# A decoder layer: the order of all engines from the end of the output projection written by hand

## Chip, cores and metric

One core of one Trainium2 chip. The metric is the device time of one launch in microseconds (us); lower is better. A run is one execution; the kernel before has three of them.

## What is computed

One decoder layer for 512 tokens of width 1024, in float32. The part that this change touches begins where the mixers have ended:

```python
def rms_norm(x, g):
    y = x * lax.rsqrt(jnp.mean(x * x, axis=-1, keepdims=True) + 1e-6)
    return y * g
...
x = x + rms_norm(mix @ w_out, post_mix_norm)          # output projection, first norm
h = rms_norm(x, pre_ffn_norm)                         # second norm
f = (jax.nn.silu(h @ w_ffn_gate) * (h @ w_ffn_up)) @ w_ffn_down
x = x + rms_norm(f, post_ffn_norm)
```

Shapes: mix 512x1024, w_out 1024x1024, w_ffn_gate and w_ffn_up 1024x2816, w_ffn_down 2816x1024.

## The kernel before

**Products in three parts.** A matmul operand is kept as a high and a low part (`hi`, `lo`, type fp32r), and a product is three matmuls: hi by hi, hi by lo, lo by hi (L270 to L272). So each weight is split after it has been loaded: ScalarE (ACT) copies it to `whi` and VectorE (DVE) writes `wlo = wraw - whi` (L135, L136). The loads go through the queue of SyncE (SP) into four buffers `wraw`; the split halves have four buffers of their own.

**Output projection and norms.** The tokens are four tiles t = 0 to 3 of 128. `wo_unit(t, i)` multiplies tile t with the i-th of eight row blocks of w_out, 6 matmuls of 512 columns into two PSUM banks (one for each half of the columns). For t = 0 and 1, blocks 0 to 5 run before the stretch shown here, blocks 6 and 7 in it. After the eight blocks of a tile comes `norms(t)`:

- ACT squares each half with a running sum (L252). DVE makes the mean `rs` (L254, L256) and multiplies the half by the gain, `py` (L260). GpSimd (POOL) raises `rs` to the power -1/2 (L258). DVE adds the scaled halves to the residual, `xr` (L264), and SP stores them to `x1d` (L267).
- For the second norm ACT squares `xr` (L863), DVE makes the mean (L224), POOL the power `rstd` (L226), and DVE writes the normed tile `hn` (L865).

`tr(t)` then turns `hn` of tile t on TensorE (PE; eight transposes, L239), ACT and DVE split the result into `h2H` and `h2L` (L127, L128), and ACT keeps a full copy `h2f` (L243). PE runs `tr(0)` inside the eight blocks of t = 2, `tr(1)` before the last block of t = 2, `tr(2)` before the last block of t = 3.

**Gate and up projection.** The first pair of column blocks is multiplied directly, first for tokens 0 to 255 (h2 of t = 0 and 1), gate then up, each in two halves i = 0 and 1 of the inner dimension, 24 matmuls of 256 columns for each; `tr(3)` stands between up i = 0 and up i = 1. Then follow the 96 matmuls for tokens 256 to 511. The remaining ten pairs run as Strassen products: from four blocks A11, A12, A21, A22 of the weights the sums S1 to S4 are formed on DVE (L920), ACT and DVE split seven operands for a pair (`unit_hi`, `unit_lo`, L944 and L952), and each unit is one product of 24 matmuls (L1016). The token side has sums too: T1 to T4 (L975), formed from `h2f` and split into `tH` and `tL`.

**What sets the order.** PE's order is written by hand throughout. The order of ACT, DVE, POOL and SP up to the Strassen products is made by the scheduler of the framework, from the program's order and dependences; from the first product on it is by hand. Each engine takes its instructions strictly in that order, SP its DMA issues too.

Of the kernel before, what the change touches and what calls it, by code (L numbers as in the profile page):

```python
# [18 lines left out]
S = 512  # L19
# [85 lines left out]
def tile_hybrid_layer(ctx: ExitStack, tc: tile.TileContext,  # L105
# [129 lines left out]
    def transpose_half(t, h, dst_hi, dst_lo, dst, half):  # L235
        p = bank("at")
        for c in range(4):
            cc = half * 4 + c
            nc.tensor.transpose(p[:, c * 128:(c + 1) * 128], h[:, cc * 128:(cc + 1) * 128], ident)  # L239
        pv = p.rearrange("p (c n) -> p c n", c=4)  # L240
        sl = (slice(None), slice(half * 4, half * 4 + 4), slice(t * 128, (t + 1) * 128))
        split_psum(pv, dst_hi[sl], dst_lo[sl])
        nc.scalar.activation(dst[sl], pv, AF.Copy)  # L243

    def post_norm(pl, po, xtile, g, dst=None, junk_of=None):
# [3 lines left out]
        for half in range(2):  # L249
            cs = slice(half * 512, (half + 1) * 512)  # L250
            junk = junk_of() if junk_of else pl.tile([128, 512], F32, name="pj")
# [703 lines left out]
    for tok in HALVES:  # L955
        for nm in ("gate", "up"):
            for i in range(2):
                if tok is HALVES[0] and nm == "up" and i == 1:
                    tr(NT - 1)
                part_fm(pss0[nm], (nm, 0), h2H, h2L, i, tok)  # L960
        if tok is HALVES[0]:
            np_.release()
            xres.release()
            gains.release()
            atp = tc.alloc_tile_pool(name="atp", bufs=1, side="left")
            aF = atp.tile([128, NF, S], F32, name="aF")
            for name in LORD:
                load_blk(0, name)
            for u in range(2):
                sums(u)  # L970
                unit_hi(u)
                unit_lo(u)
            B11, B12, B21, B22 = (h2f[:, 4 * k:4 * k + 4, tk] for k in range(2) for tk in HALVES)
            T1, T2, T3, T4 = B12, B22, B11, B21
            tsub = lambda o, a, b: V.tensor_tensor(out=o, in0=a, in1=b, op=ALU.subtract)  # L975
            tsub(T1, B12, B11)
            tsub(T2, B22, T1)
            split_sbuf(T2, tH[:, 1], tL[:, 1])
            split_sbuf(T1, tH[:, 0], tL[:, 0])
            tsub(T3, T2, B11)  # L980
            split_sbuf(T3, tH[:, 2], tL[:, 2])
            tsub(T4, B21, T2)
# [12 lines left out]
    state["fine"] = False  # L995
    for u in range(2, 5):
        sums(u)
        unit_hi(u)
        unit_lo(u)
# [77 lines left out]
    with tc.manual_schedule():  # L1077
        for u in range(NU):
            q, i = divmod(u, len(UORD))
            if i == 0:  # L1080
                cur[q] = dict(A=bank("mm"), B=bank("at"), D=bank("mm"))
            product(cur[q]["ABADADA"[i]], u, i in (0, 1, 3))
            post(u - 1)
            unit_hi(u + 5)
            if u:
                unit_lo(u + 4)
            sums(u + 6)
            if u in (NU - 5, NU - 4, NU - 1):
                pump_load(state["split"] + 4)
                pump_split(state["split"] + 1)  # L1090
            if u == NU - 2:
                split_a(2)
        post(NU - 1)
# [64 lines left out]
```

## Time and profile before

| | us |
|---|---|
| median of 3 runs (lowest to highest) | 602.11 (601.75 to 602.14) |
| the profiled execution, its own time | 604.18 |
| span of its trace, first to last instruction | 602.2 |
| PE busy in the span | 575.9 |
| DVE, ACT, POOL busy | 407.3, 302.2, 43.4 |

A row of a timeline gives start, duration, engine, line, what is written from what, how many merged, and in brackets how long the engine stood idle before it and what released it. Times run from the start of the span. A matmul's end is modelled: consecutive ones overlap, so the distance between their starts is what each costs. The granted clock of PE is given as a share of 2.4 GHz: 1.00 or 0.50 (1.2 GHz), and in between where a stretch holds both.

### The profile page before, as it was taken

The numbers are of one execution on the slowest core, as the hardware profiler recorded it, in microseconds if no ns is written. First come the engines' busy times: TensorE is split into PE (matmuls) and PEld (weight loads), VectorE is DVE, ScalarE is ACT, GpSimd is POOL, SyncE is SP. The second block draws the span as 40 slices with busy tenths as digits, with TensorE's granted clock in tenths as the row PEclk, the third lists the DMA queues.
The fourth block names the chain that finished last, engine by engine and source line by source line (L and its number), as shares of the span: only waits on it lengthen the run. The fifth ranks groups of instructions, "written<-read, shape, count | busy, mean of one in ns | idle before, by whom it ended". The sixth has DMA issues, their size and how long they took to land.

```text
span 602.2 us, 9161 instructions
## 1 busy us (share of the span) xinstructions
PE 575.9 (96%) x3554; PEld 509.2 (85%) x3554; DVE 407.3 (68%) x670; ACT 302.2 (50%) x498; POOL 43.4 (7%) x93
## 2 busy tenths in 40 slices
PE   6999898999898999979999999999999999999995
PEld 5977676888687887879999999999999988888874
DVE  5787386478888845798888788888788533323344
ACT  4656472366788935735455545545554423222231
POOL 3450001201010002010000000000000000000000
PEclk7999988999999999989999999999999999999998
DMA  8456615332322173741234323432314462332002
GB/s 307 127 143 92 147 39 139 89 114 70 97 88 71 52 260 144 220 128 37 71 106 141 106 71 106 140 109 79 112 54 146 155 251 78 106 104 83 23 36 104
DMA packets 67353, 68.45 MB, mean 114 GB/s; under 512 B 4467, under 2 KB 56726, under 8 KB 67310
## 3 DMA queue, kind: packets, MB, share of 16 engines
q1 hardware_dynamic: 66222, 65.24, 34.9%
q0 software_dynamic: 1088, 2.62, 3.0%
q8 instruction: 28, 0.46, 0.3%
q14 instruction: 15, 0.12, 0.1%
HBM read 59.99 MB, written 5.76 MB: 109 GB/s over the span
## 4 chain that ended last, share of the span: by engine, by line
PE 74%; DVE 9%; DMA 7%; ACT 5%; issue 3%; POOL 0%; SPq 0%; DVEq 0%; POOLq 0%; ACTq 0%
PE mm L1016 28%; PE mm L270 7%; PE mm L272 7%; PE mm L271 7%; DMA wraw<-in_w_in_dram 6%; PE mm L299 5%; PE at L1016 5%; PE at L270 4%; PE at L271 4%; PE at L272 4%; DVE wlo L136 3%; DMA wraw<-in_w_ffn_up_dram 1%; DVE h L384 1%; PE at L768 1%; DVE kz L687 1%
## 5 line engine op out<-in xcount | busy, mean ns | idle before, releaser
L136 DVE TENSOR_TENSOR wlo<-wraw,whi 128x512 fp32r<-128x512 f32 (+2 forms) x88 | 70.2, 820 | 53.7 <-ACT whi L135 53.6
L135 ACT ACTIVATE whi<-wraw 128x512 fp32r<-128x512 f32 (+3 forms) x92 | 63.4, 721 | 68.9 <-PE mm L272 29.6
L1016 PE MATMUL mm<-tH,wlo 128*128 128x256 f32 x240 | 67.9, 283 | 0.0
L1016 PE MATMUL mm<-tH,whi 128*128 128x256 f32 x240 | 67.8, 283 | 0.0
L1016 PE MATMUL mm<-tL,whi 128*128 128x256 f32 x240 | 67.8, 282 | 0.0
L1016 PE MATMUL mm<-h2H,whi 128*128 128x256 f32 x240 | 66.3, 276 | 0.0
L1016 PE MATMUL mm<-h2L,whi 128*128 128x256 f32 x240 | 66.3, 276 | 0.0
L1016 PE MATMUL mm<-h2H,wlo 128*128 128x256 f32 x240 | 66.3, 276 | 0.0
L944 ACT ACTIVATE whi<-sum 128x1024 fp32r<-128x1024 f32 x40 | 42.3, 1056 | 34.1 <-DVE sum L920 18.0
L270 PE MATMUL mm<-hH,whi 128*128 128x512 f32 x128 | 53.9, 421 | 0.0
L272 PE MATMUL mm<-hH,wlo 128*128 128x512 f32 x128 | 50.5, 394 | 0.0
L271 PE MATMUL mm<-hL,whi 128*128 128x512 f32 x128 | 50.4, 394 | 0.0
L952 DVE TENSOR_TENSOR wlo<-sum,whi 128x1024 fp32r<-128x1024 f32 x40 | 47.9, 1217 | 0.2 <-ACT whi L944 0.2
L1016 PEld LDWEIGHTS mm<-tH,wlo 128*128 128x128 f32 x240 | 46.0, 192 | 0.0
L1016 PEld LDWEIGHTS mm<-tH,whi 128*128 128x128 f32 x240 | 46.0, 191 | 0.0
L1016 PEld LDWEIGHTS mm<-tL,whi 128*128 128x128 f32 x240 | 46.0, 191 | 0.0
L1016 PEld LDWEIGHTS mm<-h2H,whi 128*128 128x128 f32 x240 | 45.1, 188 | 0.0
L1016 PEld LDWEIGHTS mm<-h2L,whi 128*128 128x128 f32 x240 | 45.1, 188 | 0.0
L1016 PEld LDWEIGHTS mm<-h2H,wlo 128*128 128x128 f32 x240 | 45.1, 188 | 0.0
L136 DVE TENSOR_TENSOR wlo<-aF,whi 128x1024 fp32r<-128x1024 f32 x11 | 13.4, 1224 | 35.9 <-ACT whi L135 35.9
L952 DVE TENSOR_TENSOR wlo<-wraw,whi 128x1024 fp32r<-128x1024 f32 x30 | 36.4, 1217 | 0.0
L272 PE MATMUL mm<-whi,wlo 128*128 128x512 f32 x88 | 34.4, 390 | 0.4 <-DVE wlo L136 0.4
(245 smaller groups left out, 1439.2 us busy)
## 6 DMA issues: line engine op xcount, KB each, us to landing
wraw<-in_w_ffn_down_dram SPq DMA_DIRECT2D x22, 512.0 KB, 3.3
wraw<-in_w_in_dram SPq DMA_DIRECT2D x20, 512.0 KB, 4.1
wraw<-in_w_ffn_gate_dram SPq DMA_DIRECT2D x40, 256.0 KB
wraw<-in_w_ffn_up_dram SPq DMA_DIRECT2D x40, 256.0 KB, 3.5
wraw<-in_w_out_dram SPq DMA_DIRECT2D x8, 512.0 KB, 3.2
x<-in_x_dram SPq DMA_DIRECT2D x4, 512.0 KB, 7.1
xr<-in_x_dram SPq DMA_DIRECT2D x4, 512.0 KB, 5.2
x1d<-xr SPq DMA_DIRECT2D x8, 256.0 KB, 3.3
```

The lines of the kernel that those rows point to most:

```text
L135: nc.scalar.activation(hi, t, AF.Copy)
L136: (eng or V).tensor_tensor(out=lo, in0=t, in1=hi.bitcast(F32), op=ALU.subtract)
L270: nc.tensor.matmul(ps, lhsT=lh, rhs=rh, start=start, stop=False)
L271: nc.tensor.matmul(ps, lhsT=lh, rhs=rl, start=False, stop=False)
L272: nc.tensor.matmul(ps, lhsT=ll, rhs=rh, start=False, stop=stop)
L299: nc.tensor.matmul(o, lhsT=lhs[:, cc, ts], rhs=rhs[:, c, :], start=cc == 0 and k == 0, stop=cc == DC - 1 and k == 2)
L384: V.scalar_tensor_tensor(out=h[t][:, cs], in0=xt[t][:, cs], scalar=rstd[t][:, 0:1], in1=gsb[:, cs], op0=ALU.mult, op1=ALU.mult)
L687: V.tensor_tensor(out=kz[j][half(e), e, :], in0=ps[j][half(e), :], in1=ks[half(e), e, :].bitcast(F32), op=ALU.subtract)
L768: nc.tensor.transpose(p[:, (t - kt) * 128:(t - kt + 1) * 128], P[t][:, kt * 128:(kt + 1) * 128], ident)
L944: nc.scalar.activation(hi, src[q, UORD[i]], AF.Copy)
L952: V.tensor_tensor(out=lo, in0=src[q, UORD[i]], in1=hi.bitcast(F32), op=ALU.subtract)
L1016: nc.tensor.matmul(ps, lhsT=a[:, m, c], rhs=b[:, c], start=first and m == c == k == 0, stop=c == 3 and k == 2, skip_group_check=True)
```

## The change

`norms` and `transpose_half` are taken apart into `norm_sums`, `norm_add`, `norm_next` and `tr`, `keep`; the hand-written order, which began at the first Strassen product, now begins at block 6 of t = 0, for all engines, and runs through. The split of a weight chunk of the first gate and up pair (`split_next`, four of them) is called at four written places, one instruction of 1024 columns on each engine instead of two of 512. The first Strassen blocks are loaded where the code says so, behind the last store to `x1d`, and the sums and splits of units 0 to 4 are interleaved with T1 to T4 by hand. The arithmetic and PE's order stay as they are.

```diff
-    def norms(t):
-        post_norm(np_, po[t], xt[t], g2, x1d[t * 128:(t + 1) * 128], lambda: bank("at"))
...
+    def norm_sums(t):
+        ss = small.tile([128, 2], F32, name="ss2")
+        rs = small.tile([128, 2], F32, name="rs2")
+        y = []
+        for half in range(2):
+            nc.scalar.activation(bank("at"), po[t][half], AF.Square, accum_out=ss[:, half:half + 1])
+        for half in range(2):
+            y.append(np_.tile([128, 512], F32, name="py"))
+            V.tensor_tensor(out=y[half], in0=po[t][half], in1=g2[:, half * 512:(half + 1) * 512], op=ALU.mult)
+            if half == 0:
...
+        nc.gpsimd.tensor_tensor(out=rs[:, 1:2], in0=rs[:, 0:1], in1=mhalf[:, :1], op=ALU.pow)
+        nst[t] = (y, rs)
...
+    def norm_next(t, between=None):
         hn[t] = np_.tile([128, D], F32, name="hn")
         ss = small.tile([128, 1], F32, name="ss")
         nc.scalar.activation(hn[t], xt[t], AF.Square, accum_out=ss)
+        if between:
+            between()
         rs = rstd_of(ss, 1, D)
         V.scalar_tensor_tensor(out=hn[t], in0=xt[t], scalar=rs[:, 0:1], in1=g3, op0=ALU.mult, op1=ALU.mult)
 
+    def split_next():
+        pump_load(state["split"] + 1)
+        pump_split(state["split"] + 1)
+
+    state["ahead"] = 0
+    state["fine"] = False
+    FIRST = where[("gate", 0), 0]
+    hand = tc.manual_schedule()
+    hand.__enter__()
     for t in range(2):
         for i in range(6, 8):
             wo_unit(t, i)
-        norms(t)
+        norm_sums(t)
+        if t == 0:
+            norm_add(0)
+    norm_next(0)
+    norm_add(1)
+    norm_next(1)
     for t in range(2, NT):
         po[t] = [bank("mm"), bank("mm")]
         for i in range(8):
             if i == 4 and t == 2:
                 tr(0)
-            if i == 7 and t == 2:
-                tr(1)
-            if i == 7 and t == 3:
-                tr(2)
+                keep(0)
+            if i == 7:
+                tr(t - 1)
             wo_unit(t, i)
-        norms(t)
+            if t == 3 and i in (0, 1):
+                assert state["split"] == FIRST + i
+                split_next()
+        norm_sums(t)
+        if t == 3:
+            split_next()
+        norm_add(t)
+        keep(t - 1)
+        norm_next(t, split_next if t == 3 else None)
...
+    first_pair(HALVES[0])
...
+    for name in LORD:
+        load_blk(0, name)
...
+    tsub(T1, B12, B11)
+    tsub(T2, B22, T1)
+    unit_hi(0)
+    split_sbuf(T2, tH[:, 1], tL[:, 1])
+    unit_lo(0)
+    tsub(T3, T2, B11)
+    split_sbuf(T1, tH[:, 0], tL[:, 0])
+    sums(0)
+    sums(1)
+    unit_hi(1)
+    split_sbuf(T3, tH[:, 2], tL[:, 2])
+    unit_lo(1)
+    tsub(T4, B21, T2)
+    sums(2)
+    first_pair(HALVES[1])
+    unit_hi(2)
+    unit_lo(2)
+    unit_hi(3)
+    sums(3)
+    sums(4)
+    unit_lo(3)
```

The order on DVE at the second norm of t = 0 and 1, before. `xr0` and `xr1` are the residual tiles of t = 0 and 1, `rs` with `ss` the mean of the second norm.

```order
L264 SCALAR_TENSOR_TENSOR xr1_2305<-py_2386,rs2_2382,xr1_2305 128x512
L224 TENSOR_SCALAR rs_2364<-ss_2362 128x1
L264 SCALAR_TENSOR_TENSOR xr1_2305<-py_2392,rs2_2382,xr1_2305 128x512
L224 TENSOR_SCALAR rs_2401<-ss_2399 128x1
L865 SCALAR_TENSOR_TENSOR hn_2361<-xr0_2303,rstd_2366,gain_2314 128x1024
L865 SCALAR_TENSOR_TENSOR hn_2398<-xr1_2305,rstd_2403,gain_2314 128x1024
```

And now:

```order
L224 TENSOR_SCALAR rs_2379<-ss_2377 128x1
L892 SCALAR_TENSOR_TENSOR hn_2376<-xr0_2303,rstd_2381,gain_2314 128x1024
L881 SCALAR_TENSOR_TENSOR xr1_2305<-py_2369,rs2_2364,xr1_2305 128x512
L881 SCALAR_TENSOR_TENSOR xr1_2305<-py_2373,rs2_2364,xr1_2305 128x512
L224 TENSOR_SCALAR rs_2391<-ss_2389 128x1
L892 SCALAR_TENSOR_TENSOR hn_2388<-xr1_2305,rstd_2393,gain_2314 128x1024
```

The normed tile of t = 0 now stands ahead of both residual steps of t = 1, and no longer behind the mean of t = 1.

The order on DVE from the first norm of t = 3 to its normed tile, before:

```order
L260 TENSOR_TENSOR py_2584<-mm_2513,gain_2297 128x512
L920 TENSOR_TENSOR sum_2777<-wraw_2761,wraw_2764 128x1024
L256 TENSOR_SCALAR rs2_2580<-ss2_2579 128x1
L260 TENSOR_TENSOR py_2590<-mm_2514,gain_2297 128x512
L264 SCALAR_TENSOR_TENSOR xr3_2309<-py_2584,rs2_2580,xr3_2309 128x512
L264 SCALAR_TENSOR_TENSOR xr3_2309<-py_2590,rs2_2580,xr3_2309 128x512
L952 TENSOR_TENSOR wlo_2768<-wraw_2755,whi_2767 128x1024
L952 TENSOR_TENSOR wlo_2780<-wraw_2758,whi_2779 128x1024
L224 TENSOR_SCALAR rs_2599<-ss_2597 128x1
L920 TENSOR_TENSOR sum_2901<-sum_2777,wraw_2755 128x1024
L865 SCALAR_TENSOR_TENSOR hn_2596<-xr3_2309,rstd_2601,gain_2314 128x1024
```

And now (`wraw_2318` and `wraw_2326` are the two halves of the first up block):

```order
L872 TENSOR_SCALAR rs2_2576<-ss2_2575 128x1
L869 TENSOR_TENSOR py_2585<-mm_2504,gain_2297 128x512
L136 TENSOR_TENSOR wlo_2589<-wraw_2318,whi_2588 128x1024
L881 SCALAR_TENSOR_TENSOR xr3_2309<-py_2581,rs2_2576,xr3_2309 128x512
L881 SCALAR_TENSOR_TENSOR xr3_2309<-py_2585,rs2_2576,xr3_2309 128x512
L136 TENSOR_TENSOR wlo_2602<-wraw_2326,whi_2601 128x1024
L224 TENSOR_SCALAR rs_2605<-ss_2599 128x1
L892 SCALAR_TENSOR_TENSOR hn_2598<-xr3_2309,rstd_2607,gain_2314 128x1024
```

The sums and splits of the Strassen blocks have left this stretch; the splits of the two up chunks have come into it, one ahead of the residual steps and one ahead of the mean. On ACT `whi_2601` stands behind the square of `xr3`.

The order on SP from the stores of t = 2, before, and behind it now:

```order
L911 DMA wraw_2755<-in_w_ffn_gate_dram 128x4x128
L911 DMA wraw_2755<-in_w_ffn_up_dram 128x4x128
L911 DMA wraw_2758<-in_w_ffn_gate_dram 128x4x128
L267 DMA x1d_2302<-xr2_2307 128x512 x2
L911 DMA wraw_2758<-in_w_ffn_up_dram 128x4x128
```

```order
L883 DMA x1d_2302<-xr2_2307 128x512 x2
L883 DMA x1d_2302<-xr3_2309 128x512 x2
L959 DMA wraw_2749<-in_w_ffn_gate_dram 128x4x128
L959 DMA wraw_2749<-in_w_ffn_up_dram 128x4x128
L959 DMA wraw_2752<-in_w_ffn_gate_dram 128x4x128
```

All loads of Strassen blocks now stand behind the two stores of `xr3`; before, twelve of them stood ahead.

## Rows read from the trace of the kernel before

**Rows 1.** The page, first part (busy time of each engine, share of the span, instructions) and the line by engine of the chain that ended last.

```profile
PE 575.9 (96%) x3554; PEld 509.2 (85%) x3554; DVE 407.3 (68%) x670; ACT 302.2 (50%) x498; POOL 43.4 (7%) x93
...
PE 74%; DVE 9%; DMA 7%; ACT 5%; issue 3%; POOL 0%; SPq 0%; DVEq 0%; POOLq 0%; ACTq 0%
```

**Rows 2.** Busy time in three stretches: from the end of block 3 of t = 2 to `tr(2)`, from there to `tr(3)`, and the start after it. Columns: stretch and its length, then busy us (instructions) of PE, PE's weight loads, DVE, ACT and POOL, PE's granted clock, DMA share and GB/s.

```profile
230.95:249.71 18.76, 16.96 (x82) 14.00 (x83) 13.45 (x22) 11.18 (x22) 2.50 (x3) 1.00 0.31 93
249.71:264.19 14.48, 10.64 (x86) 10.21 (x87) 10.29 (x15) 6.40 (x12) 2.00 (x2) 1.00 0.60 178
264.19:268.20 4.01, 4.01 (x21) 4.01 (x22) 3.51 (x4) 2.30 (x4) 0.00 (x0) 0.57 0.30 85
```

**Rows 3.** PE's timeline: the transposes of t = 0 to 3, the last matmul ahead of those of t = 3, and the first Strassen product.

```profile
231.69 1.06 PE L239 MATMUL at<-ident,hn 128*128 128x128 f32 x8 [0.74 <-issue]
...
236.71 1.04 PE L239 MATMUL at<-ident,hn 128*128 128x128 f32 x8
...
249.71 1.06 PE L239 MATMUL at<-ident,hn 128*128 128x128 f32 x8 [1.07 <-DVE hn L865]
...
260.08 0.28 PE L272 MATMUL at<-h2H,wlo 128*128 128x256 f32 x1
264.19 1.52 PE L239 MATMUL at<-ident,hn 128*128 128x128 f32 x8 [3.84 <-DVE hn L865]
...
280.35 0.28 PE L1016 MATMUL mm<-h2H,whi 128*128 128x256 f32 x1
```

**Rows 4.** Timelines at the second norm of t = 0 and 1: DVE's mean of t = 1 and normed tile of t = 0, and ACT's square of t = 1.

```profile
230.22 0.15 DVE L224 TENSOR_SCALAR rs<-ss 128x1 f32<-128x1 f32 x1 [1.22 <-ACT hn L863]
230.30 1.28 DVE L865 SCALAR_TENSOR_TENSOR hn<-xr,rstd,gain 128x1024 f32<-128x1024 f32 x1
...
229.04 1.06 ACT L863 ACTIVATE hn<-xr 128x1024 f32<-128x1024 f32 x1 [1.70 <-DVE xr L264]
```

**Rows 5.** SP's timeline, the issue of the second norm's gain, and the view of the gain tiles, the time of that DMA from issue to landing.

```profile
221.21 0.54 SPq L851 DMA_DIRECT2D gain<-in_pre_ffn_norm_dram  x1
...
DMA to landing us min/median/max: 8.6/8.6/8.6
```

**Rows 6.** DVE's timeline for t = 2: splits of weight chunks, the two residual steps, the normed tile.

```profile
241.57 2.49 DVE L136 TENSOR_TENSOR wlo<-wraw,whi 128x512 fp32r<-128x512 f32 x4
243.97 1.41 DVE L264 SCALAR_TENSOR_TENSOR xr<-py,rs,xr 128x512 f32<-128x512 f32 x2
...
248.28 1.28 DVE L865 SCALAR_TENSOR_TENSOR hn<-xr,rstd,gain 128x1024 f32<-128x1024 f32 x1 [0.44 <-POOL rstd L226]
```

**Rows 7.** DVE's timeline from `tr(2)`'s split to the normed tile of t = 3.

```profile
251.01 1.29 DVE L128 TENSOR_TENSOR h2L<-at,h2H 128x512 fp32r<-128x512 f32 x2 [1.44 <-ACT h2H L127]
...
255.44 1.23 DVE L920 TENSOR_TENSOR sum<-wraw 128x1024 f32<-128x1024 f32 x1 [2.39 <-DMA wraw<-in_w_ffn_up_dram]
256.58 0.21 DVE L256 TENSOR_SCALAR rs<-ss 128x1 f32<-128x1 f32 x1
...
257.44 1.42 DVE L264 SCALAR_TENSOR_TENSOR xr<-py,rs,xr 128x512 f32<-128x512 f32 x2
258.78 2.35 DVE L952 TENSOR_TENSOR wlo<-wraw,whi 128x1024 fp32r<-128x1024 f32 x2
261.05 0.14 DVE L224 TENSOR_SCALAR rs<-ss 128x1 f32<-128x1 f32 x1
...
262.76 1.28 DVE L865 SCALAR_TENSOR_TENSOR hn<-xr,rstd,gain 128x1024 f32<-128x1024 f32 x1 [0.44 <-POOL rstd L226]
```

**Rows 8.** The timelines of ACT (square of the first half of t = 3, square for its second norm) and of POOL (the power of the first norm and of the second) in the same stretch.

```profile
251.58 0.58 ACT L252 ACTIVATE at<-mm 128x512 f32<-128x512 f32 x1
...
258.89 1.06 ACT L863 ACTIVATE hn<-xr 128x1024 f32<-128x1024 f32 x1 [3.15 <-DVE xr L264]
...
256.87 0.54 POOL L258 TENSOR_TENSOR rs<-rs,mhalf 128x1 f32<-128x1 f32 x1 [8.62 <-DVE rs L256]
261.27 1.46 POOL L226 TENSOR_TENSOR rstd<-rs,mhalf 128x1 f32<-128x1 f32 x1 [3.87 <-DVE rs L224]
```

**Rows 9.** Two other waits of PE in this trace, from its timeline, and the busy time of a stretch that follows each (columns as in rows 2).

```profile
72.98 1.46 PE L606 MATMUL at<-vtok,g 128*128 128x64 f32 x8 [1.83 <-DVE g L599]
...
163.83 0.39 PE L741 MATMUL at<-ks,qs 128*128 128x256 f32 x1 [1.67 <-DVE pl L128]
...
75.00:77.00 2.00, 2.00 (x6) 1.24 (x5) 1.18 (x3) 1.96 (x3) 0.00 (x0) 0.50 0.46 130
...
163.80:168.00 4.20, 4.17 (x22) 3.52 (x23) 3.77 (x16) 2.19 (x7) 0.00 (x0) 1.00 0.01 2
```

**Rows 10.** The Strassen stage: two groups of the page (ACT's and DVE's split of a unit: busy, mean ns), DVE's T1 and T2, and from the chain in order of time a block load from issue to landing, one product of 24 matmuls, and six together.

```profile
L944 ACT ACTIVATE whi<-sum 128x1024 fp32r<-128x1024 f32 x40 | 42.3, 1056 | 34.1 <-DVE sum L920 18.0
...
L952 DVE TENSOR_TENSOR wlo<-sum,whi 128x1024 fp32r<-128x1024 f32 x40 | 47.9, 1217 | 0.2 <-ACT whi L944 0.2
...
266.99 2.54 DVE L975 TENSOR_TENSOR h2f<-h2f 128x1024 f32<-128x1024 f32 x2
...
248.70 6.56 DMA wraw<-in_w_ffn_up_dram
...
280.51 2.72 PE mm L1016 x24
...
285.95 16.80 PE mm L1016 x144
```

More of the change, by code (lines that the diff above doesn't have):

```diff
@@ L233, in square, with post_norm @@
         return ss
[L235 to L245, printed above, removed]
+    def post_norm(pl, po, xtile, g, dst=None):
         ss = small.tile([128, 2], F32, name="ss2")
@@ L250, in post_norm @@
             cs = slice(half * 512, (half + 1) * 512)
-            junk = junk_of() if junk_of else pl.tile([128, 512], F32, name="pj")
+            junk = pl.tile([128, 512], F32, name="pj")
             nc.scalar.activation(junk, po[half], AF.Square, accum_out=ss[:, half:half + 1])
@@ L851, in tile_hybrid_layer, with keep, norm_add @@
     nc.sync.dma_start(g3, pre_ffn_norm.broadcast_to([128, D]))
-    hn = {}
+    hn, nst, flips = {}, {}, {}
     def tr(t):
+        flips[t] = []
         for half in range(2):
-            transpose_half(t, hn[t], h2H, h2L, h2f, half)
-    def norms(t):
-        post_norm(np_, po[t], xt[t], g2, x1d[t * 128:(t + 1) * 128], lambda: bank("at"))
+            p = bank("at")
+            for c in range(4):
+                cc = half * 4 + c
+                nc.tensor.transpose(p[:, c * 128:(c + 1) * 128], hn[t][:, cc * 128:(cc + 1) * 128], ident)
+            pv = p.rearrange("p (c n) -> p c n", c=4)
+            sl = (slice(None), slice(half * 4, half * 4 + 4), slice(t * 128, (t + 1) * 128))
+            split_psum(pv, h2H[sl], h2L[sl])
+            flips[t].append((pv, sl))
+    def keep(t):
+        for pv, sl in flips[t]:
+            nc.scalar.activation(h2f[sl], pv, AF.Copy)
+    def norm_sums(t):
[8 more added lines that the diff above has]
+            if half == 0:
+                V.tensor_scalar(out=ss[:, 0:1], in0=ss[:, 0:1], scalar1=EPS * D, scalar2=None, op0=ALU.add)
+                V.tensor_scalar(out=rs[:, 0:1], in0=ss[:, 1:2], scalar1=ss[:, 0:1], scalar2=1.0 / D,
+                                op0=ALU.add, op1=ALU.mult)
+        nc.gpsimd.tensor_tensor(out=rs[:, 1:2], in0=rs[:, 0:1], in1=mhalf[:, :1], op=ALU.pow)
+        nst[t] = (y, rs)
+    def norm_add(t):
+        y, rs = nst[t]
+        for half in range(2):
+            cs = slice(half * 512, (half + 1) * 512)
+            V.scalar_tensor_tensor(out=xt[t][:, cs], in0=y[half], scalar=rs[:, 1:2], in1=xt[t][:, cs],
+                                   op0=ALU.mult, op1=ALU.add)
+            nc.sync.dma_start(x1d[t * 128:(t + 1) * 128, cs], xt[t][:, cs])
+    def norm_next(t, between=None):
         hn[t] = np_.tile([128, D], F32, name="hn")
@@ L954, in tile_hybrid_layer, with first_pair @@
     pss0 = {nm: [bank(tag), bank(tag)] for nm, tag in (("gate", "mm"), ("up", "at"))}
-    for tok in HALVES:
+    def first_pair(tok):
         for nm in ("gate", "up"):
@@ L959, in tile_hybrid_layer @@
                     tr(NT - 1)
+                    keep(NT - 1)
                 part_fm(pss0[nm], (nm, 0), h2H, h2L, i, tok)
[L961 to L982, printed above, removed]
+    first_pair(HALVES[0])
+    np_.release()
+    xres.release()
+    gains.release()
+    atp = tc.alloc_tile_pool(name="atp", bufs=1, side="left")
+    aF = atp.tile([128, NF, S], F32, name="aF")
+    for name in LORD:
+        load_blk(0, name)
+    B11, B12, B21, B22 = (h2f[:, 4 * k:4 * k + 4, tk] for k in range(2) for tk in HALVES)
+    T1, T2, T3, T4 = B12, B22, B11, B21
+    tsub = lambda o, a, b: V.tensor_tensor(out=o, in0=a, in1=b, op=ALU.subtract)
+    tsub(T1, B12, B11)
[19 more added lines that the diff above has]
+    unit_lo(3)
     t4 = (slice(None), slice(0, 4), HALVES[1])
@@ L994, in tile_hybrid_layer @@
         gated(j, pss0["gate"][j], pss0["up"][j])
[L995 to L999, printed above, removed]
+    unit_hi(4)
+    unit_lo(4)
     sums(5)
@@ L1075, in split_a @@
                 asp[f + j] = (hi[:, j], lo[:, j])
[L1077 to L1093, printed above, removed]
+    for u in range(NU):
+        q, i = divmod(u, len(UORD))
+        if i == 0:
+            cur[q] = dict(A=bank("mm"), B=bank("at"), D=bank("mm"))
+        product(cur[q]["ABADADA"[i]], u, i in (0, 1, 3))
+        post(u - 1)
+        unit_hi(u + 5)
+        if u:
+            unit_lo(u + 4)
+        sums(u + 6)
+        if u in (NU - 5, NU - 4, NU - 1):
+            pump_load(state["split"] + 4)
+            pump_split(state["split"] + 1)
+        if u == NU - 2:
+            split_a(2)
+    post(NU - 1)
+    hand.__exit__(None, None, None)
     fp.release()
```

## Prediction

> **What bounds the kernel now.** The page first: PE is busy for 575.9 of 602.2 us and makes 74% of the chain that ended last [rows 1]. A change that moves no work on PE can therefore gain only where PE waits or runs at its lower clock. I looked for that next, in PE's timeline over the stretch that the change touches, and read there what each wait ended on [rows 3]. There are three waits, all in front of transposes: 0.74 us before `tr(0)`, 1.07 before `tr(2)`, 3.84 before `tr(3)`. The table by stretch adds a fourth loss: behind the longest wait the granted clock is 0.57 for 4.01 us, mostly 1.2 GHz, which costs 4.01 x (1 - 0.57) = 1.72 us [rows 2]. All that the change can win is 0.74 + 1.07 + 3.84 + 1.72 = 7.4 us. From the first Strassen product on PE runs without a wait, one product in 2.72 us and six in 16.80 [rows 10], so what is won ahead of it stays won.
>
> **The first wait, `tr(0)`.** `hn` of t = 0 started at 230.30, directly behind the mean of t = 1, which had waited 1.22 us for ACT's square of t = 1 [rows 4]. Now it stands ahead of everything of t = 1. It then waits for the later of its own power and its gain. The power: mean at about 227.6, POOL 0.23 to start and 0.54 [rows 8], so 228.4. The gain was issued at 221.21 and landed 8.6 us later, at 229.8 [rows 5]. The gain decides: `hn` starts 0.45 us earlier and PE waits 0.3 instead of 0.74. The bounds are 0 (if the landing is counted from the end of the issue, 230.3) and 0.74. I take 0.45, the plain reading of the landing.
>
> The price is that both residual steps of t = 1 now queue behind this `hn`, which waits for a DMA. From 231.05: residual 1.42, square and mean 1.2 (229.04 to 230.22 [rows 4]), power 0.8, `hn` 1.28: ready at 235.8, where it was 233.3. PE comes to `tr(1)` at 236.71 - 0.45 = 236.3 [rows 3]. The cover shrinks to some 0.4 us; if it is gone, each further us is lost one for one. I take 0 and keep 0.5 as the bound.
>
> **The second wait, `tr(2)`.** Four half splits of 2.49 us stood between the products by the gain and the residual of t = 2, and more behind [rows 6]. Now all splits stand behind `hn`. Residual at about 241.7, then 1.42 + 1.2 + 0.8 + 1.28 gives `hn` at 246.4 where it was 249.6. PE arrives at 249.71 - 1.07 - 0.45 = 248.2, so the wait is gone with 1.8 us to spare: 1.07 us. The two gate chunks are then split behind it, 2 x 1.22 us [rows 10], ready at 248.9; PE wants the first at 250.5. That a chunk is split in one piece costs nothing, 1.22 us against two times 0.62 [rows 6, 10], and the full copies by `keep` lie on ACT, which was busy 11.18 of 18.76 us here and 6.40 of 14.48 in the next stretch [rows 2].
>
> **The third wait, `tr(3)`.** I count from the start of `tr(2)`, 249.71 before. PE needs 10.65 us from there to the wait (260.08 + 0.28 - 249.71), and the transposes began after 14.48 [rows 3]. That time was made of: the mean of t = 3 late (at +6.87, since a Strassen sum stood ahead and waited 2.39 us for its load), the residual, two block splits of 2.35 ahead of the next mean, and a power of 1.46 beside a DVE sum [rows 7, 8]. Now:
> - The two squares follow each other from +1.87 [rows 8], 0.7 apart, and are done at +3.2; the mean stands at +3.3, 3.6 earlier.
> - But the split of the first up half stands between the mean and the residual. ACT makes its high part behind the squares, +3.1 to +4.15 (1.06), DVE its low part to +5.4 (1.22) [rows 10]. The power is ready at +4.1, so this costs 1.3. Residual to +6.75.
> - Square to +7.95. The second split stands on ACT behind this square and on DVE ahead of the mean: high part to +9.0, low part to +10.2. The mean could have come at +8.0; this costs 2.2.
> - Power 0.23 + 0.54, with DVE quiet, instead of 1.46; `hn` 1.28 [rows 7]; 0.13 to PE: +12.45.
>
> So `tr(3)` starts 12.45 instead of 14.48 after `tr(2)`; PE waits 1.8 us instead of 3.84 and 2.03 is saved. The two splits are not in the waits of the norms here, they make them longer by 3.5. Bounds of the remaining wait: 1.4 if the handovers are as short as the shortest rows, 2.7 if the power takes 1.46 again.
>
> **The clock.** Rows stand on both sides of a wait of 1.8. After one of 1.83 the clock was 0.50; after one of 1.67 it stayed at 1.00 [rows 9]; after 1.07 it stayed as well, after 3.84 it fell [rows 2, 3]. Behind the wait of 1.83 came matmuls of 64 columns, behind that of 1.67 a dense stream of wider ones; here dense matmuls lie on both sides of the wait and the transposes, so I put it nearer to 1.67, at about 6 in 10 that the clock holds. If it holds, the 1.72 us come back too. Its bounds are 0 and 1.72.
>
> The Trainium skill, "TensorE: Matmul & The Clock Gate" (section "Why this matters for your kernels"), tells the author to avoid long idle gaps between bursts of matmuls, and by it a wait of this size leaves the clock up. By that rule the time is 596.8, the forecast below; the 1.83 of this trace speaks against taking it for certain.
>
> **What comes behind.** The Strassen loads now stand on SP behind the last store of t = 3, so the first is issued at about 255 instead of 243. Time to landing was 6.56 in the slowest row [rows 10]. Counted from the start of `tr(3)`, which is about 260.6 now: the first unit's split is wanted at +3.2 and its block lands by 262, in time; the fourth block waits for the last up split (258.4) and lands by 266, wanted by the first sum at +10.9, 271.5. DVE then has T1 to T4, six splits and four sums in a row. T1 at +2.8 as before [rows 10], 1.14 for each following operation of 1.22, and 1.1 more each time the low part waits for a high part of 1.06 that had to wait for a sum. This gives the low parts of units 2, 4 and 5 at +19.0, +24.8 and +28.2. PE without the low clock starts the first product at +14.4 (0.8 for the transposes, five times 2.72) and wants them at +20.1, +25.7 and +28.5. Cover 1.1, 0.9 and 0.3 us: it holds, by little. Before, it was some 5 us. I take 0 and keep 0.7 as the bound. If the clock falls, PE comes later and the cover is larger.
>
> **Sum.** 0.45 + 1.07 + 2.03 + 1.72 = 5.27 us off. The profiled execution took 604.18 with a span of 602.2, and the median of the three runs is 602.11; the sum is a difference inside one span, which I take off the median: 602.11 - 5.3 = 596.8.
>
> **Rivals.**
> - A, the clock falls after the 1.8 us. For it: the 1.83 [rows 9]. Then the 1.72 stays lost: 602.1 - 3.55 = 598.6.
> - B, the edit does not do what it says: splits only in the waits. If the two splits of t = 3 delay `tr(3)` by all that the mean has gained (they would have to cost 5.5 instead of the 3.5 counted), only 0.45 + 1.07 are saved and the clock falls as before: 600.6. For it: both low parts wait for a high part on ACT. Against: 1.06 and 1.22 are steady means of 40.
> - C, the Strassen operands come late with the clock up: the 0.3 of cover at unit 5 is overdrawn by some 1.5 us, spread over units 2 to 6. 598.3. For it: every estimate of a chain of twenty steps is short by something. Against: six steps of this stage follow one another without a gap before.
> - D, slower: the loads behind the store. In DVE's order everything stands behind the first Strassen sum, which needs the third and fourth block. They are issued at about 258 and have until 271.5 plus 1.1 of cover. The kernel is slower than before only if they land 5.3 us later than that, at 278, 20 us after the issue. At 22 us it would be 604. Against: 6.56 is the slowest row, and the DMA share of the stretch ahead is 0.60 [rows 2].
>
> **How the numbers follow.** Forecast 0.52, A 0.32, C 0.07, B 0.05, D 0.04. Likeliest is 596.8. Low end: the first wait gone entirely (0.3 more), a third wait of 1.4 (0.4 more) and a little on top: 595.9. High end: rival A without the 0.45 of the first wait, 599.0, and 0.3 for the thin cover of `tr(1)`: 599.3. That leaves out B and D and the far parts of the others, under 2 in 10. A measurement of this kernel can tell about 0.2%, 1.2 us, from no change: faster means under 600.9. Forecast, A and C lie under it and B is at its edge: faster 0.91, same 0.06, slower 0.03.
>
> **What would show it.** In the profile after: the wait before `tr(0)` at 0.2 to 0.4, none before `tr(1)` and `tr(2)`, one of 1.4 to 2.7 before `tr(3)`; on DVE the low part of the second up split directly ahead of the mean of t = 3; a granted clock of 1.00 or of 0.50 in the 4 us behind `tr(3)`; no idle time of PE from there to the first products of the next pair. The forecast is wrong if the wait before `tr(3)` is above 3, if `tr(1)` waits over 0.5, or if PE waits for low parts of units 2 to 6.

## The result and the profile after

The changed kernel takes 609.59 us (median of 4 runs, 608.3 to 610.19), the kernel before 602.12: ratio 1.0116, 95% interval 1.01 to 1.0133. It is slower by 7.5 us where 5.3 us less were forecast. The profiled execution took 608.3 us with a span of 606.6.

The page, first part, the line by engine of the chain that ended last, and one group of part 5 (they answer to [rows 1]):

```profile
PE 575.9 (95%) x3554; PEld 509.6 (84%) x3554; DVE 407.3 (67%) x666; ACT 301.3 (50%) x494; POOL 40.7 (7%) x93
...
PE 72%; DVE 9%; ACT 7%; DMA 7%; issue 3%; SPq 1%; POOL 1%; DVEq 0%; POOLq 0%; ACTq 0%
...
L1074 PE MATMUL mm<-tH,whi 128*128 128x256 f32 x240 | 68.7, 286 | 8.5 <-ACT cp L1084 8.5
```

PE does the same work in the same busy time. The third line is the finding: 8.5 us of PE's idle time stand in front of one group of the Strassen products, all in one piece, ended by ScalarE's copy `cp`. PE's timeline (answers to [rows 3]; L851 are the transposes `tr(0)` to `tr(3)`, L1074 the first and the third Strassen product):

```profile
230.98 1.06 PE L851 MATMUL at<-ident,hn 128*128 128x128 f32 x8 [0.26 <-issue]
...
236.01 1.04 PE L851 MATMUL at<-ident,hn 128*128 128x128 f32 x8
...
247.79 1.04 PE L851 MATMUL at<-ident,hn 128*128 128x128 f32 x8
...
260.07 1.06 PE L851 MATMUL at<-ident,hn 128*128 128x128 f32 x8 [1.39 <-DVE hn L892]
...
274.58 0.28 PE L1074 MATMUL mm<-h2H,whi 128*128 128x256 f32 x1
...
288.69 0.58 PE L1074 MATMUL mm<-tH,whi 128*128 128x256 f32 x1 [8.50 <-ACT cp L1084]
```

Up to the first Strassen product the forecast came true: 274.58 instead of 280.35, 5.77 us earlier. Two products later (at 280.19, by 288.69 - 8.50) PE wants to start the third, and there all of it and more is lost. The table by stretch of the same kernel, columns as in [rows 2]:

```profile
260.00:268.00 8.00, 7.93 (x70) 7.96 (x71) 5.33 (x6) 5.92 (x8) 0.00 (x0) 1.00 1.01 271
...
280.00:289.00 9.00, 0.50 (x3) 0.31 (x2) 7.01 (x8) 3.94 (x6) 0.00 (x0) 0.78 0.48 132
289.00:293.00 4.00, 4.00 (x24) 4.00 (x24) 4.00 (x5) 1.53 (x2) 0.00 (x0) 0.64 0.43 125
293.00:297.00 4.00, 4.00 (x35) 4.00 (x35) 2.77 (x3) 2.42 (x4) 0.00 (x0) 1.00 0.34 102
```

Behind `tr(3)` the granted clock stays at 1.00, as forecast; behind the new wait it is 0.64 for 4 us, 4 x 0.36 = 1.44 us more. 8.50 + 1.44 = 9.94 of the 10.17 us by which the span (+4.4) misses the 5.77 gained. The medians differ by 7.5, the two profiled executions by 4.1 (608.30 - 604.18), since that of before lay 2.06 above its median and that of after 1.29 below its own; where the untraced runs lose more is not shown.

### The profile page after: what moved, and what is told of

Read it like the earlier page. It is cut to its first block, busy times and chain, and to the rows that moved or that the text cites. A ratio compares the mean times of both kernels' runs of the same rounds, so it can differ in the third digit from the quotient of the medians.

```text
span 606.6 us, 9157 instructions
## 1 busy us (share of the span) xinstructions
PE 575.9 (95%) x3554; PEld 509.6 (84%) x3554; DVE 407.3 (67%) x666; ACT 301.3 (50%) x494; POOL 40.7 (7%) x93
## 4 chain that ended last, share of the span: by engine, by line
PE 72%; DVE 9%; ACT 7%; DMA 7%; issue 3%; SPq 1%; POOL 1%; DVEq 0%; POOLq 0%; ACTq 0%
PE mm L1074 28%; PE mm L260 7%; PE mm L262 7%; PE mm L261 7%; DMA wraw<-in_w_in_dram 5%; PE at L1074 4%; PE at L262 4%; PE at L260 4%; PE at L261 4%; PE mm L289 3%; DVE wlo L136 2%; DMA x<-in_x_dram 1%; PE at L758 1%; ACT whi L135 1%; ACT qs L662 1%
## 5 line engine op out<-in xcount | busy, mean ns | idle before, releaser
L135 ACT ACTIVATE whi<-wraw 128x512 fp32r<-128x512 f32 (+3 forms) x88 | 63.0, 745 | 68.0 <-PE mm L262 29.2
L1074 PE MATMUL mm<-tH,whi 128*128 128x256 f32 x240 | 68.7, 286 | 8.5 <-ACT cp L1084 8.5
L1074 PE MATMUL mm<-tL,whi 128*128 128x256 f32 x240 | 68.4, 285 | 0.0
L1074 PE MATMUL mm<-tH,wlo 128*128 128x256 f32 x240 | 68.4, 285 | 0.0
L1074 PE MATMUL mm<-h2H,whi 128*128 128x256 f32 x240 | 66.4, 276 | 0.0
L1074 PE MATMUL mm<-h2L,whi 128*128 128x256 f32 x240 | 66.3, 276 | 0.0
L1074 PE MATMUL mm<-h2H,wlo 128*128 128x256 f32 x240 | 66.3, 276 | 0.0
L992 ACT ACTIVATE whi<-sum 128x1024 fp32r<-128x1024 f32 x40 | 42.2, 1056 | 37.8 <-DVE sum L968 26.3
L1074 PEld LDWEIGHTS mm<-tH,whi 128*128 128x128 f32 x240 | 46.6, 194 | 8.7 <-ACT cp L1084 8.7
L1074 PEld LDWEIGHTS mm<-tL,whi 128*128 128x128 f32 x240 | 46.6, 194 | 0.0
L1074 PEld LDWEIGHTS mm<-tH,wlo 128*128 128x128 f32 x240 | 46.6, 194 | 0.0
L1074 PEld LDWEIGHTS mm<-h2H,whi 128*128 128x128 f32 x240 | 45.1, 188 | 0.0
L1074 PEld LDWEIGHTS mm<-h2L,whi 128*128 128x128 f32 x240 | 45.1, 188 | 0.0
L1074 PEld LDWEIGHTS mm<-h2H,wlo 128*128 128x128 f32 x240 | 45.1, 188 | 0.0
```

The source lines that it names most:

```text
L135: nc.scalar.activation(hi, t, AF.Copy)
L992: nc.scalar.activation(hi, src[q, UORD[i]], AF.Copy)
L1074: nc.tensor.matmul(ps, lhsT=a[:, m, c], rhs=b[:, c], start=first and m == c == k == 0, stop=c == 3 and k == 2, skip_group_check=True)
```

## Where the 8.5 us come from

Seven products of a pair accumulate into three PSUM banks in the order `"ABADADA"`: the third goes into the bank of the first, so ScalarE must have copied that bank out (`cp`). ScalarE's timeline of the changed kernel (L992 high parts of units 2 and 3, then 4, then 5; L135 of T4, L1051 the gate activations, L1084 the copy):

```profile
276.82 2.01 ACT L992 ACTIVATE whi<-sum 128x1024 fp32r<-128x1024 f32 x2 [5.80 <-DVE sum L968]
278.73 1.04 ACT L135 ACTIVATE h2H<-h2f 128x1024 fp32r<-128x1024 f32 x1
282.58 1.08 ACT L1051 ACTIVATE gu<-mm 128x512 f32<-128x512 f32 x2 [2.80 <-DVE h2L L136]
283.55 1.06 ACT L992 ACTIVATE whi<-sum 128x1024 fp32r<-128x1024 f32 x1
287.10 1.06 ACT L992 ACTIVATE whi<-sum 128x1024 fp32r<-128x1024 f32 x1 [2.49 <-DVE sum L968]
288.06 0.58 ACT L1084 ACTIVATE cp<-mm 128x512 f32<-128x512 f32 x1
```

The first product was done at 277.3 (274.58 + 2.72). Two things then hold the copy back. Its tile, like the gates', lies where the source of T4's split was, and the gates wait 2.80 us for that split, until 282.58. And it stands directly behind the high part of unit 5, which PE wants only three products later and which waits another 2.49 us for the sum S4. VectorE's timeline (first the low part of the second up split, the mean and `hn` of t = 3; then S1, low part of unit 2, S4, low part of unit 5):

```profile
256.69 1.23 DVE L136 TENSOR_TENSOR wlo<-wraw,whi 128x1024 fp32r<-128x1024 f32 x1 [2.17 <-ACT whi L135]
257.83 0.15 DVE L224 TENSOR_SCALAR rs<-ss 128x1 f32<-128x1 f32 x1
258.64 1.28 DVE L892 SCALAR_TENSOR_TENSOR hn<-xr,rstd,gain 128x1024 f32<-128x1024 f32 x1 [0.66 <-POOL rstd L226]
...
270.96 1.22 DVE L968 TENSOR_TENSOR sum<-wraw 128x1024 f32<-128x1024 f32 x1
...
277.91 1.23 DVE L1000 TENSOR_TENSOR wlo<-sum,whi 128x1024 fp32r<-128x1024 f32 x1 [1.19 <-ACT whi L992]
...
285.78 1.22 DVE L968 TENSOR_TENSOR sum<-wraw,sum 128x1024 f32<-128x1024 f32 x1
288.18 1.23 DVE L1000 TENSOR_TENSOR wlo<-sum,whi 128x1024 fp32r<-128x1024 f32 x1 [1.18 <-ACT whi L992]
```

The same places in the kernel before: S4 and the low part of unit 5 on VectorE, then ScalarE's high part of unit 5, gates and copy, and PE's third product.

```profile
277.85 1.22 DVE L920 TENSOR_TENSOR sum<-wraw,sum 128x1024 f32<-128x1024 f32 x1
...
281.53 1.23 DVE L952 TENSOR_TENSOR wlo<-sum,whi 128x1024 fp32r<-128x1024 f32 x1 [0.18 <-ACT whi L944]
...
280.43 1.06 ACT L944 ACTIVATE whi<-sum 128x1024 fp32r<-128x1024 f32 x1 [0.71 <-PE at L271]
281.40 1.06 ACT L990 ACTIVATE gu<-mm 128x512 f32<-128x512 f32 x2
283.27 0.60 ACT L1026 ACTIVATE cp<-mm 128x512 f32<-128x512 f32 x1 [0.80 <-PE mm L1016]
...
285.79 0.28 PE L1016 MATMUL mm<-tH,whi 128*128 128x256 f32 x1
```

The copy stood behind unit 5 there too, but harmlessly: S4 was made 13.7 us after `tr(3)` (277.85 - 264.19), now 25.7 after it (285.78 - 260.07). Nine more operations of VectorE stand between, seven that follow each other after 1.14 us and the gates' two products, which take 1.4 together: 9.4 us. They are S1 to S3 and the low parts of units 0 and 1 (these five had been done ahead of the split of `tr(3)`, most of them in the way of its norm [rows 7]), T4's low part, the two products of the gates and unit 4's low part. Most of the rest of the 12 us are VectorE's own waits for ScalarE, such as the 1.19 here.

The Trainium skill, "PSUM — Partial Sum Buffer" (section "Engine vs sequencer instructions"), says that the queues of ScalarE and VectorE are strictly first in, first out; the trace agrees: ScalarE is idle for 2.49 us ahead of unit 5's split while the copy stands behind it.

## The experiments

Theory: the wait is the copy's place in ScalarE's queue, behind splits that PE does not want yet. Rival 1: the operands are late, as the forecast's own bound had it. Rival 2: the Strassen loads, now behind the last store, land late.

**Unit 5 behind the copy.**

`post(u - 1)` stands behind product u and reads the bank of the product before it; for the first product that read is the copy.

```diff
...
         post(u - 1)
-        unit_hi(u + 5)
+        if u == 1:
+            unit_hi(5)
         if u:
+            unit_hi(u + 5)
             unit_lo(u + 4)
...
```

> Only one order on ScalarE and VectorE changes: the split of unit 5 now stands behind the copy of the first product (in the changed kernel it stands ahead of it and waits for the sum S4). Theory (the third product accumulates into the bank of the first and therefore waits for that copy, which is queued on ScalarE behind unit 5's high part): the wait in front of the third product shrinks from 8.50 us to about 5, because the copy then stands only behind the two gate activations, which wait for T4's split until 282.6, and behind unit 4's high part; time about 606, 3 to 4 us under the changed kernel. Rival 1 (the low part of unit 2 is late, VectorE's chain is too long): the order of the copy changes nothing, the wait stays at 8.5 and the time at 609.6. Rival 2 (the Strassen loads behind the last store land late): the same, 8.5 and 609.6.

605.89 us. ScalarE's timeline in this kernel, and PE's:

```profile
283.44 1.06 ACT L992 ACTIVATE whi<-sum 128x1024 fp32r<-128x1024 f32 x1
284.39 0.60 ACT L1084 ACTIVATE cp<-mm 128x512 f32<-128x512 f32 x1
286.93 1.06 ACT L992 ACTIVATE whi<-sum 128x1024 fp32r<-128x1024 f32 x1 [1.94 <-DVE sum L968]
...
285.04 0.58 PE L1074 MATMUL mm<-tH,whi 128*128 128x256 f32 x1 [4.20 <-ACT cp L1084]
```

No operand came more than 0.2 us earlier (unit 5's high part starts at 286.93, in the changed kernel at 287.10; unit 2's low part, which the third product takes, at 277.81 and 277.91), and the wait halves to 4.20. Both rivals fall.

**T4's split first.** `split_sbuf(T4, ...)` moved ahead of `unit_hi(2)`; the copy stays behind unit 5.

> T4's split (one operation on ScalarE, one on VectorE) moves ahead of the splits of units 2 and 3; the copy of the first product still stands behind unit 5's split. Theory: the gate activations, which wait for T4's split because their tile lies where its source lay, start near 279 instead of 282.6, the sum S4 and unit 5 come forward with the rest of the chain, by 1.5 to 2.1 us, and the wait in front of the third product goes from 8.50 to 6.4 to 7.0; time about 607.8. Rival 1 (the low part of unit 2 is what the third product waits for): that low part now stands behind one more operation of 1.2 us, so the wait grows to about 9.7 and the time to 610.8. Rival 2 (late loads): 8.5 and 609.6.

606.5 us, 1.3 under the expected time. PE's timeline at the third product:

```profile
286.59 0.58 PE L1074 MATMUL mm<-tH,whi 128*128 128x256 f32 x1 [6.35 <-ACT cp L1084]
```

The low part of unit 2, which rival 1 names, stands one operation later, and the wait is 2.15 shorter all the same, through the earlier S4 (283.69, in the changed kernel 285.78).

**Both, and unit 4, S4 and unit 5 behind the copy.**

```diff
...
+        if u == 1:
+            unit_hi(4)
+            unit_lo(4)
+            sums(5)
+            unit_hi(5)
+            sums(6)
...
```

> Both together: T4's split early, and unit 4, the sum S4 and unit 5 all behind the copy of the first product. Theory: gate activations near 279, copy done at 280.5 to 281, wanted by PE at 280.2: a wait of 0.3 to 1.0 before the third product instead of 8.50, and the stretches of low clock behind it are gone too; unit 2's low part is ready at 279.3 to 280.3, units 4 and 5 by 283 and 286.5, in time. Time before minus the 5.6 us by which the first product comes earlier, plus the small wait: 597 to 598.5. Rival 1 (operands late): the wait stays above 8 and the time above 608. Rival 2 (late loads): the same. A mixed case, the copy first and the operands next: the wait falls but 2 to 4 us appear before the fourth to sixth product; time 599 to 602.

601.21 us, ratio to before 0.9985 (0.9973 to 0.9998). The third product does not wait at all any more. The time is nevertheless 2.7 us above the expected range, mostly for a second wait of the same form that the expectation had missed: PE's timeline at the fifth product, and the stretch behind it.

```profile
288.04 0.39 PE L1071 MATMUL mm<-tH,whi 128*128 128x256 f32 x1 [2.11 <-ACT cp L1081]
...
288.00:292.00 4.00, 3.96 (x33) 3.96 (x34) 4.00 (x5) 1.42 (x2) 0.00 (x0) 1.00 0.47 135
```

The fifth product reuses the bank once more; the copy of the third stood behind the high parts of units 5, 6 and 7. Place and time are those of the expectation's mixed case, but it named the operands, and the wait ended on the copy.

**The two splits of t = 3 moved**, one behind the residual, one behind `hn`.

```diff
         norm_sums(t)
-        if t == 3:
-            split_next()
         norm_add(t)
+        if t == 3:
+            split_next()
         keep(t - 1)
-        norm_next(t, split_next if t == 3 else None)
+        norm_next(t)
+        if t == 3:
+            split_next()
```

> As the kernel with the copy first, and the two splits of the up half that stand in the norm of t = 3 are moved: the first behind the residual (its parts run beside the square of the next norm), the second behind the last product by the gain. Theory: the two splits cost the last transposes what the forecast counted for them, 1.3 and 2.2 us, less what the wait of PE leaves to win, so the wait before tr(3) goes from 1.39 to 0; 1.2 to 1.4 us under the kernel with the copy first, 595.7 to 597.3. Rival (the wait before tr(3) is made by the chain residual, square, power alone): it stays at 1.39 and the time is that of the kernel with the copy first. Second rival: the wait goes, and the second split, now behind the product by the gain, comes late for the second up part: a wait of 0.5 to 1.5 us there instead, same time.

600.9 us (0.9971, 0.9958 to 0.9985), 3.6 above the expected range, which started from the range of the kernel with the copy first. The wait before `tr(3)` is gone and everything from there to the fifth product is 1.3 us earlier, as expected; only 0.3 is left of it in the time. In the traced run it goes to the clock: the same wait, PE's timeline and the stretch behind it, as above.

```profile
286.73 0.39 PE L1073 MATMUL mm<-tH,whi 128*128 128x256 f32 x1 [2.12 <-ACT cp L1083]
...
286.70:290.70 4.00, 3.97 (x20) 3.98 (x21) 4.00 (x5) 1.41 (x2) 0.00 (x0) 0.57 0.45 131
```

**Both copies first.** S4 ahead of the gates' products; the high parts of units 6 to 8 behind the copies that the fifth and sixth product wait for.

> As the last kernel (copy first, splits of t = 3 moved), and what the fifth product waited for there (2.12 us, for the copy of the third, which stood on ScalarE behind the high parts of units 5, 6 and 7) is taken away in the same manner: the sum S4 stands ahead of the gates' products on VectorE, and the high parts of units 6, 7 and 8 behind the copies that the fifth and sixth product wait for. Theory (each wait in this stage is a copy queued behind a split that nobody wants yet): the 2.12 us go, and the clock stays up behind them; copies at about 278 and 284, wanted at 279 and 284.6; no wait of PE from tr(3) to the second pair; time 596.8 to 598.5, under the last kernel's 600.9 by 2.4 to 4. Rival (the operands are the next limit, since VectorE was busy 9.9 of 10 us from 270 to 280): a wait of 1 to 2 us moves to the fifth to seventh product, for a low part; time 599.5 to 601.

598.59 us (0.9937, 0.9921 to 0.9953), within 0.1 of the expected range. The 2.12 are gone; a wait of 1.16 is left at the seventh product, for VectorE's sum `gu` that reads the fifth product's bank, and one of 0.18 in the second pair. PE's timeline:

```profile
290.34 0.39 PE L1074 MATMUL mm<-h2H,whi 128*128 128x256 f32 x1 [1.16 <-DVE gu L1088]
```

**That sum first as well**, ahead of the low part of unit 8 and the next pair's S2.

> As the kernel with both copies first; in it the seventh product waited 1.16 us for VectorE's sum that reads the bank of the fifth (that sum stood behind the low parts of units 6 to 8 and a sum of the next pair). Here the low part of unit 8 and that sum of the next pair stand behind it. Theory (same form as before: a read of a bank queued behind splits that nobody wants yet): the wait of 1.16 goes or falls under 0.3, no other appears; time 597.2 to 598, under the kernel with both copies first by 0.6 to 1.3. Rival (VectorE is full in this stage, so whatever is put back is late for the next pair): a wait of 0.7 to 1.2 appears in the second pair; same time.

601.52 us (0.999, 0.9976 to 1.0005): worse by 2.9 than the kernel with both copies first. The rival was right in form, though not in size. The 1.16 are gone and a wait of 2.97 has come at the third product of the second pair, again for the copy of its first product, which stands behind the second S4's split:

```profile
300.49 0.58 PE L1074 MATMUL mm<-tH,whi 128*128 128x256 f32 x1 [2.97 <-ACT cp L1084]
```

The next pair's S2, put back, had pushed that S4 back, from 296.05 to 297.57.

**In every pair** the high part that waits for S4 stands behind the first copy. Against the kernel with that sum first:

```diff
...
         elif u:
-            unit_hi(u + 5)
+            if i == 1:
+                unit_hi(u + 4)
+            if i:
+                unit_hi(u + 5)
             unit_lo(u + 4)
...
```

> As the kernel with the gate's sum first, in which the wait went to the second pair: its third product waited 2.97 us for the copy of its first, queued on ScalarE behind the high part that waits for the second S4. Here this copy stands ahead of that high part in every pair. Theory: the 2.97 us go (the first product of the second pair ends at 294.8 and its copy needs 0.6), and no wait over 0.3 is left from tr(3) to the end of the products; time 597 to 598.3. Rival (VectorE is full, an operand is next): the seventh or eighth later product waits 1 to 3 us for a low part; time 599 to 601.5.

596.85 us, 0.9915 (0.9895 to 0.9934), just under the expected range: the best version, 12.7 under the changed kernel. All of PE's waits from 225 us to 480, past the end of the Strassen products, in the view of waits:

```profile
PE at L851 <- issue: 0.4, 1, 0.4
```

**Only the middle by hand**: the norms as the scheduler sets them, the hand-written order from the first gate and up parts on.

> The norms as in the kernel before, set by the scheduler, and the hand-written order only from the first gate and up parts on, as in the changed kernel. Theory (the hand-written order of the Strassen part alone makes the wait of 8.50, since in it the sums S1, S2, S3 and the splits of units 0 and 1 no longer stand ahead of the last transposes): the wait before tr(2) of about 1 stays, tr(3) comes without the sums in its norm with a wait of 0 to 1, and the third product waits 8 to 9 us for the copy of the first; time 608 to 610. Rival (the hand-written norms cause it, by the later loads): the third product waits under 1 us; time about 597 to 599.

610.2 us, as the theory had it but for 0.2; the wait of the third product is a little over the expected 8 to 9. PE's timeline (`tr(2)`, `tr(3)`, third product):

```profile
249.40 1.06 PE L239 MATMUL at<-ident,hn 128*128 128x128 f32 x8 [1.16 <-DVE hn L865]
...
259.89 1.04 PE L239 MATMUL at<-ident,hn 128*128 128x128 f32 x8
...
289.56 0.58 PE L1028 MATMUL mm<-tH,whi 128*128 128x256 f32 x1 [9.58 <-ACT cp L1038]
```

`tr(3)` does not wait at all, with the scheduler's norms. So the gain at `tr(3)` does not need the hand-written norms: taking the Strassen sums and splits out of its way is enough. The same step makes the wait of the third product. The Strassen loads are issued from 242.48 on here, as in the kernel before, and not from 254.96 as in the changed one: late loads are not what PE waits for.

**Only the norms by hand**, the Strassen part ahead of the products by the scheduler.

> The norms by hand as in the changed kernel; the hand-written order ends ahead of the first gate and up parts, and the scheduler sets the order of the Strassen part as in the kernel before (the product loop is by hand in both). The scheduler puts the low parts of units 0 and 1 between the residual of t = 3 and its next mean. Theory: no wait before tr(1) and tr(2); before tr(3) 1.4 plus the two low parts, 2.3, so 3.7 to 4.5 us with a low clock behind it; S4 stands behind one split of T4 and the gates, so the copy of the first product is ready about 22.3 us after tr(3), wanted at 20.1: a wait of 1.5 to 3 before the third product; time 600 to 603. Rival (the norms' order alone brings what the forecast said): no wait over 0.5 before the third product and 596 to 598.

600.03 us (0.9956, 0.9939 to 0.9973). VectorE's low parts of units 0 and 1, and PE's `tr(3)` and third product:

```profile
254.56 2.35 DVE L1000 TENSOR_TENSOR wlo<-wraw,whi 128x1024 fp32r<-128x1024 f32 x2
...
260.32 1.06 PE L851 MATMUL at<-ident,hn 128*128 128x128 f32 x8 [1.52 <-DVE hn L892]
...
281.69 0.38 PE L1066 MATMUL mm<-tH,whi 128*128 128x256 f32 x1 [0.51 <-ACT cp L1076]
```

My expectation of 3.7 to 4.5 before `tr(3)` was wrong: the two low parts lie in the 2.17 us in which VectorE otherwise waits for the high part of the second up split, and cost 0.13. So this is a wait of the norms in which a split does stand free of charge, and two operations fewer are left for the stretch behind `tr(3)`. The wait of the third product is 0.51 where 1.5 to 3 was expected; that the norms' order alone brings 596 to 598 is not borne out.

**The same with the splits of t = 3 moved.**

> Norms by hand, Strassen part by the scheduler, as in the kernel of that kind that ran at 600.03; the two splits of t = 3 are moved, the first behind the residual, the second behind the last product by the gain. The scheduler then also puts only one unit's low part ahead of that product. Theory: the wait of 1.52 before tr(3) shrinks to under 0.6; the sums stand later in the order that the scheduler now makes (S2 and S3 behind the splits of T), S4 behind three low parts, so the copy of the first product, still behind unit 5's split, comes later than there: a wait of 2 to 5 before the third product where that kernel had 0.51; time 600 to 604. Rival (what is won at tr(3) is kept): no more than 0.5 before the third product, time 598.4 to 599.

602.41 us (1.0013, 1.0001 to 1.0024). `tr(3)` no longer waits; counted from it (257.02, without the moved splits 260.32), S4 now starts 20.9 us later instead of 18.5, and the third product waits. ScalarE's timeline (high part of unit 5, copy) and PE's:

```profile
279.24 1.06 ACT L994 ACTIVATE whi<-sum 128x1024 fp32r<-128x1024 f32 x1 [3.76 <-DVE sum L970]
280.20 0.58 ACT L1078 ACTIVATE cp<-mm 128x512 f32<-128x512 f32 x1
...
280.83 0.58 PE L1068 MATMUL mm<-tH,whi 128*128 128x256 f32 x1 [3.72 <-ACT cp L1078]
```

The theory's ranges held, 2 to 5 us for the wait and 600 to 604 for the time: what is won at `tr(3)` is lost behind it.

## Why the prediction was wrong

- `tr(0)`: forecast 0.3, measured 0.26; `hn` waited for the gain's landing, as said.
- `tr(1)`: no wait; `hn` ends at 235.52 (234.24 + 1.28) and PE comes at 236.01, a cover of 0.49 where 0.4 was counted. `tr(2)`: no wait, as forecast.
- `tr(3)`: 12.28 us after `tr(2)` (260.07 - 247.79) where 12.45 was counted. The second low part ends at +10.13 (forecast +10.2). The wait is 1.39, just under the range of 1.4 to 2.7 and 0.4 under the 1.8 of the forecast, in part because PE's work from `tr(2)` to the wait took 10.89 (12.28 - 1.39) instead of 10.65. That the two splits make it longer was right; moving them takes it away.
- Clock behind `tr(3)`: 1.00, the forecast case. Rival A did not happen, nor D: the first Strassen sum starts with no wait for its loads.
- Sum to the first product: 0.48 + 1.07 + 2.45 + 1.72 = 5.72 by these rows, 5.77 by its start, 5.27 forecast.
- **The failed step is "What comes behind".** For the third product its times were right: PE wants it at +20.1, forecast and measured (280.19 - 260.07), and unit 2's low part ends at +19.07 (forecast +19.0). Units 4 and 5 end at +25.8 and +29.3 (forecast +24.8 and +28.2), 1.0 and 1.1 late, which is more than their cover of 0.9 and 0.3: against the +25.7 and +28.5 at which the forecast has PE want them, some 0.8 us of rival C, hidden here behind the longer wait. The 8.50 us themselves are of another kind, since the step asked only when the operands are ready. A product also needs its bank, and the bank's reader stood on ScalarE behind unit 5's high part, at +27.0 to +28.1, and behind T4's split. "I take 0 and keep 0.7 as the bound" was a bound on the wrong thing. The kernel before showed what was needed: the copy directly behind unit 5's split and gates, and by my own count unit 5's low part, at +28.2, came some 10 us later than before, relative to `tr(3)` (+18.6: 281.53 + 1.23 - 264.19). None of the three signs that were named for a wrong forecast appeared; what did was idle time of PE at a place where none was to be.
- "What is won ahead of it stays won" leaned on the stage of before having no wait; that held only while five operations of VectorE were done ahead of it. With them ahead, `tr(3)` waited 3.84 us [rows 3]; with them behind, the third product waits 8.50, and the kernel with only the middle by hand shows both ends of this exchange by themselves.

With every copy ahead of the splits that are not wanted yet, the kernel runs at 596.85, where 596.8 was forecast. That is partly chance: it also holds the 1.3 us of the moved splits, which the forecast left in the wait, and against the runs of the kernel before that were taken beside it (601.63) it is 4.8 us less, not 5.3.

## What to carry to other kernels

For each matmul group behind a moved stretch, list two times: when its operands are ready, and when its accumulator bank has been read; then look at what stands ahead of that reader in its engine's queue. In a hand-written order, a read that frees a bank goes ahead of splits that are wanted later, above all of those that wait for something themselves. Work that delays one wait may be the work that prevents the next: before taking it out of a wait, count where its results are due.

## What was not expected of the hardware

- Two waits of PE at the same place with nearly the same length, 2.11 and 2.12 us, left the granted clock at 1.00 in one kernel and at 0.57 over the next 4 us in the other. The length of a wait does not by itself tell what follows.
- POOL's power takes 0.54 to 0.56 us in all seven places from 227 us on in the changed kernel, where VectorE stands idle beside it or multiplies out of PSUM; it took 1.46 beside a sum of VectorE in the kernel before [rows 8]. POOL's timeline after, t = 3, first and second norm:

```profile
251.49 0.54 POOL L874 TENSOR_TENSOR rs<-rs,mhalf 128x1 f32<-128x1 f32 x1 [7.27 <-DVE rs L872]
258.06 0.54 POOL L226 TENSOR_TENSOR rstd<-rs,mhalf 128x1 f32<-128x1 f32 x1 [6.03 <-DVE rs L224]
```

In the kernel before, three more powers of the second norm were longer too:

```profile
228.42 0.98 POOL L226 TENSOR_TENSOR rstd<-rs,mhalf 128x1 f32<-128x1 f32 x1 [0.93 <-DVE rs L224]
...
230.45 1.53 POOL L226 TENSOR_TENSOR rstd<-rs,mhalf 128x1 f32<-128x1 f32 x1 [1.05 <-DVE rs L224]
...
247.33 0.92 POOL L226 TENSOR_TENSOR rstd<-rs,mhalf 128x1 f32<-128x1 f32 x1 [5.66 <-DVE rs L224]
```

Each of the four long powers of the kernel before starts while VectorE works from SBUF, and each ends 0.40 or 0.41 us after that operation: at 229.40, 231.98, 248.25 and 262.73, the operations (a residual step, `hn`, a split, a sum) at 229.00, 231.58, 247.85 and 262.32.

The Trainium skill, "SBUF — State Buffer" (section "SBUF: two separate sides"), describes the port pair that VectorE and GpSimd share as an exclusive lock, not a split of bandwidth. The durations and these ends fit that; no run here separated it from other causes.
